# The order of the first loads, and two branch chunks moved behind a recurrence's last product

## The chip, the cores and the metric

The kernel runs on one core of a Trainium2 chip. The metric is the device time of one execution in microseconds (us); lower is better. The profile comes from one execution recorded by the hardware profiler; its engines are TensorE (PE, with its weight loads PEld), VectorE (DVE), ScalarE (ACT), GpSimd (POOL) and SyncE (SP), which here only issues DMAs.

## The reference

One layer of a hybrid encoder on x of 1024 rows by 1024 channels and a memory of 256 rows, all in float32:

```
h = rmsnorm(x);  z = h @ w_in                       # one projection, split into
(hq, hf, hi, hg, fq, fk, fv, ff, mq, gate_logits)   # parts of three mixers and three gates
y_a = hgrn2(hq, hf, hi, hg)      # gated linear recurrence, 4 heads, 128 x 128 state
y_b = fox(fq, fk, fv, ff)        # forgetting attention, 8 heads x 64, causal
y_c = memory_attention(mq, rmsnorm(mem) @ mem_kv_w) # 4 heads x 128 over 256 rows
merged = sum over b of sigmoid(gate_b) * (y_b @ w_br_b)
x = x + merged @ w_out
x = x + conv_glu_ffn(rmsnorm(x)) # up 1024 -> 2 x 2816, causal conv of 3, gelu, down
```

The recurrence's output is normalised per row and head and multiplied by silu(hg).

## The kernel before

Activations lie transposed: 128 channels on the partitions, the 1024 rows of the sequence along the free dimension, in eight tiles `xk[0]` to `xk[7]`. A float32 product is made from three TensorE products (`mm3`): both operands are split into a high part (a cast by ScalarE, L120, or L276 for x with its norm gain) and a low part (a subtraction by VectorE, L128 or L277), and high-high, high-low and low-high are added in PSUM (L114, L115, L116). One such product has 128 x 128 weights and 512 columns.

**The first part.** SyncE issues all loads in the order of the program. Memory (`mt`, 1 MB, transposed), the key-value weights of the memory (`wkv[0]` to `wkv[7]`, 512 KB each; 0 to 3 are for keys, 4 to 7 for values), x, the weights of the first two gate chunks (`rgw`, 512 KB each), and the rows of memory and of x, which are only needed for the sums of squares of the norms. The computing steps go by a list written out by hand, `SEQ`:

- `k0` to `k7` (`kv_chunk`): split one chunk of key-value weights, then 12 products on the normed memory; the result of the keys lies in two `tr` banks of PSUM, that of the values in two `pp` banks.
- `x0` to `x7` (`x_chunk`): scale and split 128 channels of x into `uh` and `ul`.
- `g0`, `g1` (`gate_weights`): split the weights of a gate chunk.
- `s0` to `s7` (`gate_step`): 12 products of both gate chunks on one channel tile of x.
- `mn` (`mem_norm`), `mk` (`mem_keys`): the keys are normed by ScalarE and VectorE (L326 to L331), turned by eight transposes (L336) and evicted into `mkf` (L338). `mv` (`mem_values`): ScalarE evicts the values from PSUM into `mvf` (L318).
- `xn` (`x_norm`): eight squares with sums by ScalarE, one for each row tile of x (L356), then the reciprocal root.

Behind the list comes the stream of dense projections. It uses banks of the same PSUM pools: `pp` has three, `tr` and `lg` two, `po` one. After the splits ScalarE also rescales the tiles of x (L542) in eight steps for a Strassen-like family of products; four are tied to the last split of x (`late["x_cast"]`), four to the last square (`late["square"]`).

A scheduler decides the order on each engine from priorities; the program's order is the base, and `tc.issue_after(ins)` ties instructions behind another one.

**The recurrence and the branches.** `hgrn_mix(h, ya)` runs one head in two halves of 512 rows (n = 0, 1). A half has a preparation (transposes of `kE`, L1033, products L1038), the products with the running state (L1044, L1046, with the states updated by VectorE at L1050 and L1052), and then `finish`: a square (L1060), a sum (L1061), four scalings by ScalarE (L1064), four transposes (L1067) and the multiplication by the gate (L1068). `state["last"]` is the last product with the state. A `finish` is held over and called inside the next half; the last one is called by the main program.

`branch(br, yh, yl, js)` projects a mixer's output: each chunk j is 24 products (two halves of the sequence, four channel tiles, three products each) whose result is multiplied by the gate (L1135) into `merged`. `weave` takes steps of several generators in turn, by their fractions done; `chain`, `held` and `ahead` join generators and give them priorities. The lines that the change meets are:

```
weave((ahead(hgrn_mix(3, ya), AHEAD), HGRN_STEPS), (chain(branch(1, yh, yl, range(2)), held(branch(1, yh, yl, range(2, 7)), 2)), 14))
state.pop("finish")()
with tc.issue_after(state["last"].ins):
    run_all(branch(1, yh, yl, (7,)))
```

So chunks 0 to 6 of branch 1 are woven with head 3 of the recurrence, and chunk 7 is tied behind its last product.

Of the kernel before, what the change touches and what calls it, by code (L numbers as in the profile page):

```python
# [8 lines left out]
F32 = mybir.dt.float32  # L9
# [25 lines left out]

FOX_STEPS, HGRN_STEPS, MEM_STEPS = 28, 14, 7
AHEAD = 300
FOX_LATE = 0.2  # L40
SEQ = ("k0 k1 k2 k3 x0 x1 g0 x2 mr g1 k4 s0 s1 x3 s2 k5 x4 mn mk s3 k6 x5 s4 k7 mv x6 s5 x7 xn s6 s7").split()
TMIN = -(1.0 - 2.0 ** -24)


# [13 lines left out]
def weave(*parts):  # L58

    live = [[g, max(n, 1), s[0] if s else 0.0, 0] for g, n, *s in parts]  # L60
    while live:
        p = min(live, key=lambda q: q[2] + (1.0 - q[2]) * q[3] / q[1])
        try:
            next(p[0])
            p[3] += 1
        except StopIteration:
            live.remove(p)
# [3 lines left out]
def tile_block(ctx: ExitStack, tc: tile.TileContext, xT, memT, x_rows, mem_rows, vec, fbias, mats, hmask, w_cm, w_hi, w_fqk, w_fv,  # L71
# [26 lines left out]
    def col(i):  # L98
        return cv[:, i:i + 1]


    def ahead(gen, offset):

        while True:
            with tc.high_priority(offset) if offset else nullcontext():
                try:
                    next(gen)
                except StopIteration:
                    return
            yield  # L110

    def mm3(ps, lh, ll, rh, rl, first, last, more=False):

        PE.matmul(ps, lh, rh, start=first, stop=False, skip_group_check=more)  # L114
        PE.matmul(ps, lh, rl, start=False, stop=False, skip_group_check=more)  # L115
        PE.matmul(ps, ll, rh, start=False, stop=last, skip_group_check=more)  # L116

    def cast(eng, out, in_):
        if eng is S:
# [6 lines left out]
    def split(eng, h, l, src, sub=None):  # L126
        cast(eng, h, src)
        return (sub or V).tensor_sub(l, src, h.bitcast(F32))  # L128

    def rstd_small(out, ss, n):  # L130
        w = ss.shape[1]
        V.tensor_scalar(out, ss, 1.0 / n, EPS, ALU.mult, ALU.add)
        return G.tensor_tensor(out, out, mhalf[:, :w], ALU.pow)
# [3 lines left out]
    def raw_weights(src, n):  # L137
        raw = wp.tile([P, 4 * 264], F32, tag="raw", name="raw", bufs=2)
        SP.dma_start(raw[:, :n], src)
        return raw  # L140

    def weights(src, shape, raw=None, hl=None, parts=1):

        n = shape[0] * shape[1]
        if raw is None:
            raw = raw_weights(src, n)
        if hl is None:
            hl = [wp.tile([P, 4 * 264], F32R, tag=t, name=t, bufs=3) for t in ("wh", "wl")]
        for i in range(parts):
            sl = slice(i * n // parts, (i + 1) * n // parts)  # L150
            split(wsplit[0], hl[0][:, sl], hl[1][:, sl], raw[:, sl], wsplit[1])
        return [t[:, :n].rearrange("p (a b) -> p a b", a=shape[0]) for t in hl]
# [43 lines left out]
    def row_tile(name):  # L196
        return p0.tile([P, 2 * HB], F32, tag="wkv", name=name, bufs=6)

    wkv = [row_tile(f"wkv{q}") for q in range(4)]
    mem_row = [row_tile(f"mr{i}") for i in range(2)]  # L200
    wkv += [row_tile(f"wkv{q}") for q in range(4, 8)]
    x_row = [row_tile(f"xr{i}") for i in range(6)]
    x_row += [row_tile(f"xr{i}") for i in (6, 7)]
    SP.dma_start(cv, vec)
    for q in range(4):
        w = 2 if q else 1
        for i in range(2 // w):
            sl, ws = slice(2 * q + i, 2 * q + i + w), slice(i * HB, (i + w) * HB)
            SP.dma_start(mt[:, sl, :], memT[:, sl, :])
            SP.dma_start(wkv[q][:, ws], w_mkv[q][:, ws])  # L210
    SP.dma_start(ones, mats[:, P:2 * P])
    rgw = []
    for what in SEQ:
        if what[0] == "x" and what != "xn":
            k = int(what[1])
            SP.dma_start(xk[k], xT[:, k, :])
        elif what == "mr":
            for i in range(2):
                SP.dma_start(mem_row[i], mem_rows[i])
        elif what[0] == "g":  # L220
            br, j = order[int(what[1])]
            rgw.append(raw_weights(w_cm[16 + 8 * br + j], KC * P))
        elif what in ("k4", "k5", "k6", "k7"):
            q = int(what[1])
            SP.dma_start(wkv[q], w_mkv[q])
    SP.dma_start(ident, mats[:, 0:P])
    for i in range(8):
        last_row = SP.dma_start(x_row[i], x_rows[i])
    G.memset(mhalf, -0.5)
    warm = cp.tile([P, 1], F32, tag="warm", name="warm")  # L230
    S.activation(warm, mhalf[:, 0:1], AF.Exp)
# [29 lines left out]

    umh = p0.tile([P, KC, NM], F32R, tag="umh", name="umh")
    uml = p0.tile([P, KC, NM], F32R, tag="uml", name="uml")
    for k in range(KC):
        S.activation(umh[:, k, :], mt[:, k, :], AF.Copy, scale=col(C_GM + k))
        V.scalar_tensor_tensor(out=uml[:, k, :], in0=mt[:, k, :], scalar=col(C_GM + k),
                               in1=umh[:, k, :].bitcast(F32), op0=ALU.mult, op1=ALU.subtract)
    rm = p0.tile([P, 2], F32, tag="rm", name="rm")

    def mem_norm():  # L270
# [2 lines left out]
        rstd_small(rm, rm, D)  # L273

    def x_chunk(k):
        late["x_cast"] = S.activation(uh[k], xk[k], AF.Copy, scale=col(C_GX + k))  # L276
        V.scalar_tensor_tensor(out=ul[k], in0=xk[k], scalar=col(C_GX + k), in1=uh[k].bitcast(F32),  # L277
                               op0=ALU.mult, op1=ALU.subtract)

    def spread_dma(r, rcol, pool, name):  # L280

# [22 lines left out]
    def kv_chunk(i):  # L304

        what, q = i // 4, i % 4
        if q == 0:
            pkv[what] = [ps_proj(), ps_proj()] if what else [ps_tr(), ps_tr()]
        wh, wl = weights(None, (2, HB), wkv[i], parts=1 if i else 2)
        for kk in range(2):  # L310
            k = 2 * q + kk
            for m in range(2):
                ms = slice(m * P, (m + 1) * P)
                mm3(pkv[what][m], umh[:, k, ms], uml[:, k, ms], wh[:, kk, :], wl[:, kk, :], k == 0, k == KC - 1)
# [27 lines left out]
    gw, gps = [], []  # L342

    def gate_weights(i):
        gw.append(weights(None, (KC, P), rgw[i], [p0.tile([P, KC * P], F32R, tag=t, name=t) for t in (f"gh{i}", f"gl{i}")]))
        gps.append([ps_proj(), ps_po()] if i else [ps_lg(), ps_lg()])

    def gate_step(k):
# [2 lines left out]
                sl = slice(n * HB, (n + 1) * HB)  # L351
                mm3(gps[i][n], gw[i][0][:, k, :], gw[i][1][:, k, :], uh[k][:, sl], ul[k][:, sl], k == 0, k == KC - 1)

    def x_norm():
        for i in range(8):
            late["square"] = S.activation(x_row[i], x_row[i], AF.Square, accum_out=rt[:, i:i + 1])  # L356
        rstd_small(rt, rt, D)

    steps = dict(k=kv_chunk, x=x_chunk, g=gate_weights, s=gate_step)
    named = dict(mn=mem_norm, mk=mem_keys, mv=mem_values, xn=x_norm)  # L360
    for what in SEQ:
        if what == "mr":
            continue
        if what in named:
            named[what]()
        else:
            steps[what[0]](int(what[1]))
    p0.release()

    home = {}  # L370
# [560 lines left out]
    def hgrn_mix(h, ya):  # L931
# [7 lines left out]
        for n in range(2):  # L939
# [113 lines left out]
                                               op0=ALU.mult, op1=ALU.add)  # L1053
                    St = Sn

            def finish(po=po, gz=gz, sl=sl):

                o2 = ph.tile([P, 4, P], F32, tag="o2", name="o2")
                rr = ph.tile([P, 4], F32, tag="rr", name="rr", bufs=2)
                S.activation(o2, po.rearrange("p (b v) -> p b v", b=4), AF.Square)  # L1060
                V.reduce_sum(rr, o2, axis=AX.X)  # L1061
                state["norm"] = rstd_small(rr, rr, 4 * P)
                for b in range(4):
                    S.activation(o2[:, b, :], po[:, b * P:(b + 1) * P], AF.Copy, scale=rr[:, b:b + 1])  # L1064
                ptr = ps_tr()
                for b in range(4):
                    PE.transpose(ptr[:, b * P:(b + 1) * P], o2[:, b, :], ident)  # L1067
                V.scalar_tensor_tensor(out=ya[:, h, sl], in0=ptr, scalar=hgc, in1=gz[:, sl], op0=ALU.mult, op1=ALU.mult)  # L1068

            state["finish"] = finish  # L1070
# [53 lines left out]
    def branch(br, yh, yl, js=range(8)):  # L1124
        for j in js:
            i = order.index((br, j))
            gts = []
            for n in range(2):
                gt = gate_tile()
                SP.dma_start(gt, gd[i, n])  # L1130
                gts.append(gt)
            for n, ps in br_chunk(br, j, yh, yl):
                dst = merged(j, n)
                if i < 8:
                    V.scalar_tensor_tensor(out=dst, in0=gts[n], scalar=1.0, in1=ps, op0=ALU.add, op1=ALU.mult)  # L1135
                else:
                    V.scalar_tensor_tensor(out=gts[n], in0=gts[n], scalar=1.0, in1=ps, op0=ALU.add, op1=ALU.mult)
                    V.tensor_add(dst, dst, gts[n])
                yield

    weave((ahead(hgrn_mix(3, ya), AHEAD), HGRN_STEPS), (chain(branch(1, yh, yl, range(2)), held(branch(1, yh, yl, range(2, 7)), 2)), 14))
    state.pop("finish")()
    with tc.issue_after(state["last"].ins):
        run_all(branch(1, yh, yl, (7,)))
    state["ph"].release()
# [509 lines left out]
```

## Time and profile before

| | us |
|---|---|
| median of 3 runs (lowest, highest) | 1734.2 (1732.5, 1734.95) |
| the profiled execution | 1735.67 |
| its span on the core | 1733.9 |
| TensorE busy | 1714.0 |
| VectorE busy | 1144.5 |
| ScalarE busy | 808.3 |
| GpSimd busy | 322.8 |

The span is what the timeline shows; 1.77 us of the profiled execution lie outside it. A row of the timeline gives start, duration, engine, line, operation, the tiles written and read, shapes and count, and in brackets how long the engine was idle before it and which engine, tile and line released it. "SPq" is the issue of a DMA. Where several rows overlap on one engine, the distance of their starts is what each one costs.

### The profile page before, as it was taken

Reading aid. Unit: us, or ns where it says so; the run is one execution under the profiler, and the core shown is the slowest. Engines: PE = TensorE matmul, PEld = TensorE weight load, DVE = VectorE, ACT = ScalarE, POOL = GpSimd, SP = SyncE. Lnnn points to the kernel's source line nnn. Section 1 sums busy time; section 2 is a strip of 40 time slices with the busy share of each in tenths; the row PEclk is TensorE's granted clock in tenths of the full one; section 3 lists DMA queues with packets and bytes.
Section 4 is the critical chain, followed back from the end, with each engine's and each line's share of the span. In section 5 each row is a group of like instructions: output and inputs, shape, how many; then the busy total and the mean of one; then the engine's idle time right before and its main releaser. Section 6 shows DMA issues by size and latency. Waiting matters only on the chain.

```text
span 1733.9 us, 24255 instructions
## 1 busy us (share of the span) xinstructions
PE 1714.0 (99%) x8941; PEld 1452.6 (84%) x8941; DVE 1144.5 (66%) x2046; ACT 808.3 (47%) x1436; POOL 322.8 (19%) x417
## 2 busy tenths in 40 slices
PE   8999999999999999999989999999999999999998
PEld 6778899989898998888878888788888888888887
DVE  7656545665666564886856745987777787765654
ACT  8634346645454553776531333644334344433332
POOL 0100022443433331544210000211111111100000
PEclk9999999999999999999999999999999999999999
DMA  9533142221212111100336542565445345494772
GB/s 358 179 123 115 66 137 86 76 90 44 98 62 79 55 50 56 61 31 24 111 113 199 162 182 97 158 172 168 138 148 140 116 133 152 159 348 157 249 264 85
DMA packets 83207, 227.23 MB, mean 131 GB/s; under 512 B 9600, under 2 KB 12424, under 8 KB 83088
## 3 DMA queue, kind: packets, MB, share of 16 engines
q1 hardware_dynamic: 65040, 161.19, 26.8%
q0 software_dynamic: 18048, 64.50, 12.8%
q8 instruction: 70, 1.15, 0.3%
q14 instruction: 49, 0.40, 0.1%
HBM read 180.78 MB, written 67.93 MB: 143 GB/s over the span
## 4 chain that ended last, share of the span: by engine, by line
PE 96%; DMA 2%; DVE 1%; SPq 0%; issue 0%; ACT 0%; POOL 0%; DVEq 0%; POOLq 0%; ACTq 0%
PE pp L116 21%; PE pp L115 21%; PE pp L114 21%; PE lg L116 4%; PE lg L115 4%; PE lg L114 4%; PE tr L115 2%; PE tr L116 2%; PE tr L114 2%; PE po L836 1%; PE lg L795 1%; PE lg L794 1%; PE po L835 1%; PE po L116 1%; PE po L114 1%; PE po L115 1%
## 5 line engine op out<-in xcount | busy, mean ns | idle before, releaser
L116 PE MATMUL pp<-uh,wl 128*128 128x512 f32 x412 | 164.4, 399 | 0.0
L115 PE MATMUL pp<-ul,wh 128*128 128x512 f32 x412 | 164.4, 399 | 0.0
L114 PE MATMUL pp<-uh,wh 128*128 128x512 f32 x412 | 163.6, 397 | 0.0
L115 PE MATMUL pp<-wl,uh 128*128 128x256 f32 (+1 forms) x512 | 145.9, 286 | 0.0
L116 PE MATMUL pp<-wh,ul 128*128 128x256 f32 (+1 forms) x512 | 145.6, 285 | 0.0
L114 PE MATMUL pp<-wh,uh 128*128 128x256 f32 (+1 forms) x512 | 145.1, 285 | 0.0
L120 ACT CAST wh<-s 128x512 fp32r<-128x512 f32 x113 | 68.3, 619 | 157.7 <-PE pp L115 84.9
L120 ACT CAST wh<-raw 128x1024 fp32r<-128x1024 f32 (+2 forms) x76 | 67.6, 890 | 111.6 <-PE pp L115 95.5
L120 ACT CAST wh<-rw 128x512 fp32r<-128x512 f32 x87 | 53.2, 619 | 104.7 <-PE pp L115 62.1
L1300 POOL DMA_DIRECT2D rw<-in_w_up x44 | 24.2, 556 | 399.4 <-DVE wl L1193 178.4
L114 PEld LDWEIGHTS pp<-wh,uh 128*128 128x128 f32 x512 | 96.7, 189 | 1.2
L116 PEld LDWEIGHTS pp<-wh,ul 128*128 128x128 f32 x512 | 96.8, 189 | 0.9
L115 PEld LDWEIGHTS pp<-wl,uh 128*128 128x128 f32 x512 | 96.7, 189 | 0.9
L128 DVE TENSOR_TENSOR wl<-raw,wh 128x1024 fp32r<-128x1024 f32 (+2 forms) x75 | 78.1, 1041 | 28.8 <-ACT wh L120 28.3
L120 ACT CAST dwh<-wr 128x1024 fp32r<-128x1024 f32 (+1 forms) x41 | 40.1, 979 | 118.5 <-PE tr L115 39.7
L114 PEld LDWEIGHTS pp<-uh,wh 128*128 128x128 f32 x412 | 78.0, 189 | 15.7 <-ACT wh L120 0.3
L115 PEld LDWEIGHTS pp<-ul,wh 128*128 128x128 f32 x412 | 77.5, 188 | 15.8
L116 PEld LDWEIGHTS pp<-uh,wl 128*128 128x128 f32 x412 | 77.5, 188 | 15.7
L128 DVE TENSOR_TENSOR dwl<-wr,dwh 128x1024 fp32r<-128x1024 f32 (+1 forms) x41 | 46.3, 1129 | 34.0 <-ACT dwh L120 33.9
L810 ACT ACTIVATE pt<-pt,st 128x128 f32<-128x128 f32 (+3 forms) x64 | 49.7, 777 | 40.0 <-DVE st L807 33.1
L812 POOL TENSOR_SCALAR pt<-pt,st 128x128 f32<-128x128 f32 (+3 forms) x64 | 51.1, 798 | 78.0 <-DVE st L811 59.9
L120 ACT CAST ph<-tr 128x512 fp32r<-128x512 f32 (+1 forms) x80 | 41.7, 544 | 39.8 <-PE tr L824 17.6
(500 smaller groups left out, 5145.3 us busy)
## 6 DMA issues: line engine op xcount, KB each, us to landing
rw<-in_w_up POOLq DMA_DIRECT2D x44, 512.0 KB, 4.6
sd<-in_w_dn POOLq DMA_DIRECT2D x30, 512.0 KB, 5.9
br<-yd SPq DMA_DIRECT2D x30, 512.0 KB, 5.3
raw<-in_w_cm SPq DMA_DIRECT2D x26, 512.0 KB, 3.4
gd<-gt SPq DMA_DIRECT2D x48, 256.0 KB, 2.0
gt<-gd SPq DMA_DIRECT2D x48, 256.0 KB, 2.7
yd<-fc SPq DMA_DIRECT2D x44, 256.0 KB, 2.4
wr<-sd SPq DMA_DIRECT2D x20, 512.0 KB, 5.0
```

The costliest lines, as they stand in the source:

```text
L114: PE.matmul(ps, lh, rh, start=first, stop=False, skip_group_check=more)
L115: PE.matmul(ps, lh, rl, start=False, stop=False, skip_group_check=more)
L116: PE.matmul(ps, ll, rh, start=False, stop=last, skip_group_check=more)
L120: return S.copy(out, in_)
L128: return (sub or V).tensor_sub(l, src, h.bitcast(F32))
L794: PE.matmul(ps[:, :w], qa[i][:, tsl], kh[i][:, s0:s0 + w], start=True, stop=False)
L795: fox_sets[p][3] = PE.matmul(ps[:, :w], qa[i][:, tsl], kl[i][:, s0:s0 + w], start=False, stop=True)
L810: S.activation(pt[:, :ns], pt[:, :ns], AF.Exp, bias=st[:, 2:3], accum_out=st[:, 3:4])
L812: G.tensor_scalar(pt[:, :ns], pt[:, :ns], st[:, 3:4], 0.0, ALU.mult, ALU.add)
L835: PE.matmul(o, vhl[:, sb, :], ph[:, src], start=(sb == 0), stop=False)
L836: PE.matmul(o, vhl[:, sb, :], pl[:, src], start=False, stop=last)
L1300: late["raw"] = G.dma_start(raw[:, 2 * i:2 * i + 2, :], src[:, 2 * i:2 * i + 2, :])
```

## The change

The first loads come in a new order, written as a list of its own (`LOADS`): gate weights and channels of x, then the memory, its rows, the key-value weights and the rows of x. The computing list `SEQ` follows: all eight gate steps first, then the memory's operand, the eight key-value chunks and the norms. The first gate's weights and the first tile of x are loaded and split in two pieces each (256 and 768 columns; 512 and 512), the first key-value chunk in one instead of two. The squares of x are single steps in the list. In the other place chunk 6 of branch 1 leaves the weave and is issued behind the recurrence's last product, and the last four transposes of `finish` are tied behind chunk 6's last product (`late["mm"]`, kept by `mm3`); chunk 7 follows as before.

```diff
-SEQ = ("k0 k1 k2 k3 x0 x1 g0 x2 mr g1 k4 s0 s1 x3 s2 k5 x4 mn mk s3 k6 x5 s4 k7 mv x6 s5 x7 xn s6 s7").split()
+LOADS = "g0 x0 g1 x1 x2 x3 x4 x5 x6 x7 m mr k0 k1 k2 k3 k4 k5 xr0 xr1 xr2 xr3 k6 k7 xr4 xr5 xr6 xr7".split()
+SEQ = ("g0 x0 g1 s0 x1 s1 x2 s2 x3 s3 x4 s4 x5 s5 x6 s6 x7 s7 m k0 mn k1 k2 k3 k4 xr0 k5 xr1 xr2 mk xr3 k6 xr4 k7 xr5 "
+       "mv xr6 xr7 xn").split()
...
-        PE.matmul(ps, ll, rh, start=False, stop=last, skip_group_check=more)
+        late["mm"] = PE.matmul(ps, ll, rh, start=False, stop=last, skip_group_check=more)
...
+    for what in LOADS:
+        i = int(what[-1]) if what[-1].isdigit() else None
+        if what[:2] == "xr":
+            x_row[i] = row_tile(what)
+            last_row = SP.dma_start(x_row[i], x_rows[i])
+        elif what[0] == "x":
+
+            sl = slice(0 if i else HB, T)
+            SP.dma_start(xk[i][:, sl], xT[:, i, sl])
+        elif what[0] == "g":
+            br, j = order[i]
+            rgw[i] = wp.tile([P, 4 * 264], F32, tag="raw", name="raw", bufs=2)
+            for sl in (slice(0, 2 * P), slice(2 * P, KC * P)) if i == 0 else (slice(0, KC * P),):
+                SP.dma_start(rgw[i][:, sl], w_cm[16 + 8 * br + j][:, sl])
+                if i == 0 and sl.start == 0:
+                    SP.dma_start(xk[0][:, :HB], xT[:, 0, :HB])
...
-    def x_norm():
-        for i in range(8):
-            late["square"] = S.activation(x_row[i], x_row[i], AF.Square, accum_out=rt[:, i:i + 1])
-        rstd_small(rt, rt, D)
+    def x_square(i):
+        late["square"] = S.activation(x_row[i], x_row[i], AF.Square, accum_out=rt[:, i:i + 1])
...
-            def finish(po=po, gz=gz, sl=sl):
+            def finish(after=None, po=po, gz=gz, sl=sl):
...
-                for b in range(4):
-                    PE.transpose(ptr[:, b * P:(b + 1) * P], o2[:, b, :], ident)
+                with tc.issue_after(after.ins) if after is not None else nullcontext():
+                    for b in range(4):
+                        PE.transpose(ptr[:, b * P:(b + 1) * P], o2[:, b, :], ident)
...
-    weave((ahead(hgrn_mix(3, ya), AHEAD), HGRN_STEPS), (chain(branch(1, yh, yl, range(2)), held(branch(1, yh, yl, range(2, 7)), 2)), 14))
-    state.pop("finish")()
+    weave((ahead(hgrn_mix(3, ya), AHEAD), HGRN_STEPS), (chain(branch(1, yh, yl, range(2)), held(branch(1, yh, yl, range(2, 6)), 2)), 12))
+
+    with tc.issue_after(state["last"].ins):
+        run_all(branch(1, yh, yl, (6,)))
+    state.pop("finish")(late["mm"])
     with tc.issue_after(state["last"].ins):
         run_all(branch(1, yh, yl, (7,)))
```

More of the change, by code (lines that the diff above doesn't have):

```diff
@@ L197, in row_tile @@
         return p0.tile([P, 2 * HB], F32, tag="wkv", name=name, bufs=6)
[L199 to L203, printed above, removed]
-    SP.dma_start(cv, vec)
[L205 to L216, printed above, removed]
+    wkv, mem_row, x_row, rgw = {}, {}, {}, {}
+    SP.dma_start(cv, vec)
+    for what in LOADS:
[13 more added lines that the diff above has]
+                    SP.dma_start(xk[0][:, :HB], xT[:, 0, :HB])
+        elif what == "m":
+            for sl in (slice(0, 4), slice(4, 8)):
+                SP.dma_start(mt[:, sl, :], memT[:, sl, :])
@@ L217, in tile_block @@
         elif what == "mr":
             for i in range(2):
+                mem_row[i] = row_tile(f"mr{i}")
                 SP.dma_start(mem_row[i], mem_rows[i])
[L220 to L225, printed above, removed]
+            SP.dma_start(ones, mats[:, P:2 * P])
+        else:
+            wkv[i] = row_tile(what)
+            SP.dma_start(wkv[i], w_mkv[i])
@@ L226, in tile_block @@
     SP.dma_start(ident, mats[:, 0:P])
-    for i in range(8):
-        last_row = SP.dma_start(x_row[i], x_rows[i])
     G.memset(mhalf, -0.5)
@@ L263, in tile_block, with memory_operand @@
     uml = p0.tile([P, KC, NM], F32R, tag="uml", name="uml")
[L264 to L267, printed above, removed]
+    def memory_operand():
+        for k in range(KC):
+            S.activation(umh[:, k, :], mt[:, k, :], AF.Copy, scale=col(C_GM + k))
+            V.scalar_tensor_tensor(out=uml[:, k, :], in0=mt[:, k, :], scalar=col(C_GM + k),
+                                   in1=umh[:, k, :].bitcast(F32), op0=ALU.mult, op1=ALU.subtract)
     rm = p0.tile([P, 2], F32, tag="rm", name="rm")
@@ L275, in x_chunk @@
     def x_chunk(k):
-        late["x_cast"] = S.activation(uh[k], xk[k], AF.Copy, scale=col(C_GX + k))
-        V.scalar_tensor_tensor(out=ul[k], in0=xk[k], scalar=col(C_GX + k), in1=uh[k].bitcast(F32),
-                               op0=ALU.mult, op1=ALU.subtract)
+        for sl in [slice(0, HB), slice(HB, T)] if k == 0 else [slice(0, T)]:
+            late["x_cast"] = S.activation(uh[k][:, sl], xk[k][:, sl], AF.Copy, scale=col(C_GX + k))
+            V.scalar_tensor_tensor(out=ul[k][:, sl], in0=xk[k][:, sl], scalar=col(C_GX + k),
+                                   in1=uh[k][:, sl].bitcast(F32), op0=ALU.mult, op1=ALU.subtract)
     def spread_dma(r, rcol, pool, name):
@@ L308, in kv_chunk @@
             pkv[what] = [ps_proj(), ps_proj()] if what else [ps_tr(), ps_tr()]
-        wh, wl = weights(None, (2, HB), wkv[i], parts=1 if i else 2)
+        wh, wl = weights(None, (2, HB), wkv[i])
         for kk in range(2):
@@ L344, in gate_weights @@
     def gate_weights(i):
-        gw.append(weights(None, (KC, P), rgw[i], [p0.tile([P, KC * P], F32R, tag=t, name=t) for t in (f"gh{i}", f"gl{i}")]))
+        hl = [p0.tile([P, KC * P], F32R, tag=t, name=t) for t in (f"gh{i}", f"gl{i}")]
+        for sl in (slice(0, 2 * P), slice(2 * P, KC * P)) if i == 0 else (slice(0, KC * P),):
+            split(S, hl[0][:, sl], hl[1][:, sl], rgw[i][:, sl])
+        gw.append([t.rearrange("p (a b) -> p a b", a=KC) for t in hl])
         gps.append([ps_proj(), ps_po()] if i else [ps_lg(), ps_lg()])
@@ L352, in gate_step @@
                 mm3(gps[i][n], gw[i][0][:, k, :], gw[i][1][:, k, :], uh[k][:, sl], ul[k][:, sl], k == 0, k == KC - 1)
-    def x_norm():
-        for i in range(8):
-            late["square"] = S.activation(x_row[i], x_row[i], AF.Square, accum_out=rt[:, i:i + 1])
-        rstd_small(rt, rt, D)
-    steps = dict(k=kv_chunk, x=x_chunk, g=gate_weights, s=gate_step)
-    named = dict(mn=mem_norm, mk=mem_keys, mv=mem_values, xn=x_norm)
+    def x_square(i):
+        late["square"] = S.activation(x_row[i], x_row[i], AF.Square, accum_out=rt[:, i:i + 1])
+    steps = dict(k=kv_chunk, x=x_chunk, g=gate_weights, s=gate_step, xr=x_square)
+    named = dict(m=memory_operand, mn=mem_norm, mk=mem_keys, mv=mem_values, xn=lambda: rstd_small(rt, rt, D))
     for what in SEQ:
-        if what == "mr":
-            continue
         if what in named:
@@ L366, in tile_block @@
         else:
-            steps[what[0]](int(what[1]))
+            steps[what[:-1]](int(what[-1]))
     p0.release()
```

## The prediction

> **What bounds the kernel now.** I read the page's span and busy lines first, then TensorE's waits, then the timeline around the two places that the change touches.
>
> ```profile
> span 1733.9 us, 24255 instructions
> ...
> PE 1714.0 (99%) x8941; PEld 1452.6 (84%) x8941; DVE 1144.5 (66%) x2046; ACT 808.3 (47%) x1436; POOL 322.8 (19%) x417
> ```
> ```profile
> PE tr L114 <- ACT wh L120: 6.4, 2, 5.2
> PE tr L1067 <- ACT o L1064: 3.9, 1, 3.9
> PE pp L116 <- DVE fa L1392: 1.7, 1, 1.7
> ```
>
> TensorE is busy for 1714.0 of 1733.9 us, so 19.9 us is all that any reordering of unchanged work can win. The waits say where those lie: 6.4 us at the start (5.2 before the first product and one more), 3.9 us at L1067, 1.7 us in the FFN, which the change does not touch. A reader should see two things: the change touches the first two places, and everything else that it moves lies where TensorE does not wait today, so that it can only lose there.
>
> The profiled execution took 1735.67 us, 1.47 above the median of the runs (1734.2). I make the sum against the span and add it to the median.
>
> **The start.** The number of products before the dense projections is the same before and after (96 for the gates, 96 for keys and values, 8 transposes). What counts is how late TensorE runs against an uninterrupted stream.
>
> ```profile
> 2.58 0.43 SPq L210 DMA_DIRECT2D wkv<-in_w_mkv  x1
> 3.06 0.43 SPq L209 DMA_DIRECT2D mt<-in_memT  x1
> 3.53 0.43 SPq L210 DMA_DIRECT2D wkv<-in_w_mkv  x1
> ...
> 5.18 1.22 PE L114 MATMUL tr<-wh,umh 128*128 128x512 f32 x2 [5.18 <-ACT wh L120]
> ...
> 6.36 0.62 ACT L120 CAST wh<-wkv 128x512 fp32r<-128x512 f32 x1 [0.82 <-DMA wkv<-in_w_mkv]
> ...
> 7.05 0.63 PE L115 MATMUL tr<-wl,umh 128*128 128x512 f32 x1
> ...
> 7.48 0.63 PE L116 MATMUL tr<-wh,uml 128*128 128x512 f32 x1
> ...
> 8.56 0.91 ACT L265 ACTIVATE umh<-mt,cv 128x256 fp32r<-128x256 f32 x2 [1.58 <-DMA mt<-in_memT]
> ...
> 9.83 1.04 ACT L120 CAST wh<-wkv 128x1024 fp32r<-128x1024 f32 x1 [0.36 <-DMA wkv<-in_w_mkv]
> ...
> 10.91 1.23 DVE L128 TENSOR_TENSOR wl<-wkv,wh 128x1024 fp32r<-128x1024 f32 x1 [0.92 <-ACT wh L120]
> 10.93 0.74 PE L114 MATMUL tr<-wh,umh 128*128 128x512 f32 x2 [1.17 <-ACT wh L120]
> ...
> 12.19 0.50 PE L115 MATMUL tr<-wl,umh 128*128 128x512 f32 x1 [0.52 <-DVE wl L128]
> ...
> 25.26 0.50 PE L116 MATMUL po<-uh,gl 128*128 128x512 f32 x1 [0.27 <-DVE gl L128]
> ```
>
> The unit of the stream is below: twelve 512-wide products start at 52.30 and the thirteenth at 55.11, so 2.81 us for twelve and 0.234 for one. At 12.19 fourteen products are done, worth 3.28 us; TensorE has then lost 12.19 − 3.28 = 8.91 us, and 0.27 more at 25.26: 9.2 us.
>
> In the changed kernel the first loads are gate weights 128 KB, half of x's first channels 256 KB, the rest of the weights 384 KB, the other half 256 KB, then the second gate's weights 512 KB. Before they are 128, 256, 128, 256, 256 and 512 KB of memory and key weights. So at equal bytes the first product is cast as early (5.2), the fourth product waits for what 1 MB brings (before, 8.56), and the second gate's weights come with 1.5 MB (cast at 9.83, its low part subtracted 10.91 to 12.14). The built order on TensorE is six products of gate 0, then four of gate 1 that need no low part, then two that do. So ten products are done at 12.2 where before fourteen were: the loss is 12.19 − 10 × 0.234 = 9.85 us, **0.7 later**. Bounds: each load of equal bytes is issued one slot earlier (2.58, 3.06 and 3.53 are 0.47 apart), and if the chain follows that and the 0.27 is not met again elsewhere, the start is 0.9 earlier; if the clock, cold at first (7.05 to 7.48 is 0.43 for one product against 0.234), stays cold for some 3.5 us longer because TensorE now idles between the third product and the fourth, it is 0.7 + 1.7 = 2.4 later. I take +0.7, since the bytes are equal.
>
> **The end of this part.** Here is the term that I think decides. Before, the last steps were gate steps; the eviction of the memory values (L318) ran under them. After, the key and value chunks are last.
>
> ```profile
> 23.88 1.27 ACT L326 ACTIVATE mkt<-tr,rm 128x512 f32<-128x512 f32 x2
> 25.04 1.04 ACT L120 CAST wh<-wkv 128x1024 fp32r<-128x1024 f32 x1
> 25.97 1.16 ACT L327 ACTIVATE mkt<-mkt 128x512 f32<-128x512 f32 x2
> ...
> 46.59 1.04 ACT L356 ACTIVATE xr<-xr 128x1024 f32<-128x1024 f32 x1
> ...
> 47.63 1.04 ACT L356 ACTIVATE xr<-xr 128x1024 f32<-128x1024 f32 x1
> ...
> 48.67 0.67 ACT L318 ACTIVATE mvf<-pp,rm 128x512 f32<-128x512 f32 x1
> ...
> 54.41 4.25 ACT L542 ACTIVATE xk<-xk,cv 128x1024 f32<-128x1024 f32 x4
> ```
> ```profile
> 37.92 1.04 PE L336 MATMUL tr<-ident,mkt 128*128 128x128 f32 x8
> 38.72 0.48 PE L116 MATMUL pp<-wh,uml 128*128 128x512 f32 x1
> ...
> 52.30 0.39 PE L114 MATMUL lg<-uh,gh 128*128 128x512 f32 x1
> ...
> 55.11 0.39 PE L114 MATMUL pp<-uh,wh 128*128 128x512 f32 x1
> ```
>
> The product at 55.11 is the first of the dense projections. In the changed kernel its PSUM bank is that of the first value half, so it waits for ScalarE's first L318. ScalarE works in order, and in the built kernel its order from the end of the fourth key chunk on is (lines of the kernel before):
>
> ```
> L326 mkt x2 (needs the fourth key chunk's products)
> L356 square; L327 x2; L120 cast k6, k7; L356; L120 raw
> L356 x2; L120 raw; L356
> L542 rescale of x, channels 4 to 7
> L318 mvf x2
> ```
>
> By the rows that is 1.16 (L326, 23.88 to 25.04) + 5 × 1.04 (squares) + 1.16 (L327) + 4 × 0.93 (casts, 25.04 to 25.97) + 4.25 (L542) + 0.67 (the first L318) = **16.2 us**. TensorE meanwhile has four value chunks of twelve products, 11.2 us, and the eight transposes, 0.80 (37.92 to 38.72): **12.0 us**. So it waits 16.2 − 12.0 = **4.2 us** where before it waited for nothing (the row at 55.11 has no wait). ScalarE itself is not late before this chain: from 11 us to the chain's start at 9.85 + 144 × 0.234 = 43.6 it has some 26 us of casts and squares. Bounds: rows overlap by about 0.1 each, and the scheduler's list is fixed, so 3.5; 5.0 if a row of x comes late. Behind the waiting product, TensorE's whole dense stream is queued, so all of it is paid. The eviction of the keys (L338) and the transposes of the row norms come after, under that stream, at no cost as long as it covers them; uncovered it would be two evictions, 1.3 us, in the upper bound.
>
> **What the wait does to the clock.** The trace has one idle time of this size, and one short one.
>
> ```profile
> 889.20:893.60 4.40, 0.48 (x4) 0.25 (x3) 2.72 (x6) 1.77 (x5) 1.01 (x1) 0.89 0.39 119
> 893.57:899.97 6.40, 5.96 (x29) 5.67 (x30) 1.79 (x4) 1.20 (x4) 0.00 (x0) 0.54 0.00 0
> ```
>
> These are windows of all engines; the columns are length, busy time of TensorE, its weight loads, VectorE, ScalarE and GpSimd, then granted clock. While TensorE idles the mean clock is 0.89, and after it 0.54: 3.92 us of idling cost the clock about (1 − 0.54) × 6.4 = 2.9 us. The 1.17 us at 10.93 did not (its stream goes on at full pitch after 12.19). A wait of 4.2 us is nearest to the first. I take +1.7: half of 3.5 us of cold stream, the length of the start's cold stretch, since here a dense stream follows at once; bounds 0 (clock kept) and 2.9.
>
> The Trainium skill ("TensorE: Matmul & The Clock Gate", Part 1, the HAM clock gate) says that the clock halves only after a whole idle window of about 3.4 us and that these windows run freely, whatever the kernel does. By that an idle time of 4.2 us holds a whole window only in about (4.2 − 3.4) / 3.4, a quarter, of its positions, and the sum would more often be 1.7 lower; the trace's one case of 3.92 us did drop.
>
> **The branch part.** The weave now holds chunks 0 to 5 of branch 1, and chunk 6's 24 products go behind the recurrence's last product (L1046 of the last half), the last four transposes behind these, then chunk 7.
>
> ```profile
> 882.48 0.48 PE L116 MATMUL pp<-yh,wl 128*128 128x512 f32 x1
> ...
> 889.26 0.38 PE L1046 MATMUL po<-St,qe 128*128 128x128 f32 x2
> 893.57 0.48 PE L1067 MATMUL tr<-ident,o 128*128 128x128 f32 x1 [3.92 <-ACT o L1064]
> ...
> 906.52 0.60 PE L1067 MATMUL tr<-ident,o 128*128 128x128 f32 x4
> ```
> ```profile
> 882.99 0.69 DVE L1135 SCALAR_TENSOR_TENSOR mgl<-gt,pp 128x512 f32<-128x512 f32 x1
> 883.60 0.68 DVE L128 TENSOR_TENSOR wl<-raw,wh 128x512 fp32r<-128x512 f32 x1
> 884.20 0.34 DVE L1052 SCALAR_TENSOR_TENSOR St<-St,eg,tr 128x128 f32<-128x128 f32 x1
> ...
> 890.67 0.68 DVE L1061 TENSOR_REDUCE rr<-o 128x4 f32<-128x512 f32 x1
> ```
> ```profile
> 889.74 0.60 ACT L1060 ACTIVATE o<-po 128x512 f32<-128x512 f32 x1 [0.34 <-PE po L1046]
> ```
>
> L1067 occurs twice. The wait of 3.92 us at 893.57 belongs to the *first* half of head 3; the recurrence's products of the second half follow it. The last transposes are those at 906.52, and they have no wait: chunk 7 already covers them. So chunk 6 gains nothing at its new place. At its old place it lay between 882.79 and 889.2, between the last products of the first half, and covered their chain of states on VectorE. Without it the last product would start 24 × 0.234 = 5.6 earlier, at 883.65; but VectorE starts the first state (L1052) at 884.20, behind L1135 and L128, and three of them at 0.34 less some overlap end at about 885.1. So it starts some 1.4 later than the move alone allows. The finishing chain behind (L1060, L1061) gains back up to 0.3, as L1061, ready at 889.74 + 0.60 = 890.34, had to wait until 890.67 for VectorE. Net **+1.1**: TensorE idles about as long in all, no work having come to the stall. Bounds: 0 and +2; and if the idle time in one piece falls to 3.6 us and the clock stays up, the 2.9 us above come back: −1.8.
>
> **Sum.** 0.7 + 4.2 + 1.7 + 1.1 = +7.7 us: 1734.2 + 7.7 = **1741.9 us**.
>
> **Rivals.** *No cold clock at either place:* 0.7 + 4.2 + 1.1 − 2.9 = +3.1, 1737.3. For it: 4.2 and 3.6 us are close to what the one observed drop needed; against it, that drop. *All upper bounds:* start 2.4, wait 5.0, clock 2.0, branch 1.1: +10.5, 1744.7. *The other side:* ScalarE reaches L318 in time. It decides at the four rescalings: if they do not stand ahead of L318 in effect (because the squares before them finish under earlier idle time), the chain is 16.2 − 4.25 = 12.0 us, as long as TensorE's, and there is neither wait nor drop. Then +1.8 remains, 1736.0; with the branch's clock kept, −1.1, 1733.1; with the start's early bound too, −2.7, 1731.5. Against it: ScalarE's order is fixed in the built kernel, and L326 cannot start before the fourth key chunk ends. *The change does not do what it says:* the last transposes had no wait to cover; that is in the sum already.
>
> **How the numbers follow.** Some 0.2%, 3.5 us, is what a measurement of this kernel can tell from no change. Forecast, with or without one of the two clock terms (+4.8 to +7.7): 0.64, slower. Upper bounds (+9 to +11): 0.10, slower. No cold clock anywhere (+2 to +3.5): 0.16, the same. ScalarE in time: 0.10, of it 0.08 the same and 0.02 faster; faster gets 0.03 with the chance of something unseen, the same 0.23. The range leaves out most of the last case and the top of the upper bounds: 1736.0 to 1745.5.
>
> **What would show it.** In the profile after, TensorE's waits would list the first dense product (pp, L114 of before) on ScalarE's mvf with about 4 us, a granted clock near one half right behind it, L1067 with 3.5 to 4 us still there, and ten products done at about 12.2 us. If the mvf wait is under 1 us, the forecast is wrong at its main term; if L1067's wait is gone or under 2 us, at the branch.

## The result, and the profile after

| | before | after |
|---|---|---|
| median of 6 runs, us | 1733.8 (1732.5 to 1734.95) | 1739.79 (1739.29 to 1740.68) |
| the profiled execution, its span | 1735.67, 1733.9 | 1739.85, 1738.1 |

The changed kernel is slower: the ratio is 1.0035, 95% interval 1.0022 to 1.0048, that is 3.8 to 8.3 us; the medians differ by 6.0. The forecast was +7.7, 1741.9 with a range of 1736.0 to 1745.5.

The page after, and TensorE's waits after (engine, product and line, what released it: us in total, times, longest). Lines of the changed kernel stand three to ten higher than before: L117 to L119 are the three products, L325 is the value eviction, L548 the rescaling of x, L1074 the transposes of the recurrence's output.

```profile
span 1738.1 us, 24251 instructions
...
PE 1714.7 (99%) x8941; PEld 1451.9 (84%) x8941; DVE 1144.5 (66%) x2047; ACT 808.5 (47%) x1437; POOL 324.4 (19%) x417
```
```profile
PE lg L117 <- ACT uh L283: 6.7, 2, 5.3
PE pp L117 <- ACT mvf L325: 4.3, 1, 4.3
PE tr L1074 <- ACT o L1070: 3.6, 1, 3.6
PE pp L119 <- DVE fa L1402: 1.6, 1, 1.6
PE po L1052 <- DVE St L1058: 1.2, 2, 0.8
```

TensorE does the same work (1714.7 against 1714.0). The list of waits has one new large line, the value eviction, and the wait at the recurrence's transposes is still there: 3.6 us instead of 3.9.

The new wait, on ScalarE and on TensorE:

```profile
44.27 1.25 ACT L333 ACTIVATE mkt<-tr,rm 128x512 f32<-128x512 f32 x2
...
55.45 4.25 ACT L548 ACTIVATE xk<-xk,cv 128x1024 f32<-128x1024 f32 x4
59.60 1.24 ACT L325 ACTIVATE mvf<-pp,rm 128x512 f32<-128x512 f32 x2
```
```profile
55.02 1.03 PE L343 MATMUL tr<-ident,mkt 128*128 128x128 f32 x8
60.32 0.51 PE L117 MATMUL pp<-uh,wh 128*128 128x512 f32 x1 [4.27 <-ACT mvf L325]
```

The rows of ScalarE from 44.27 to 59.60 follow each other without a pause. From the first read of the keys out of PSUM at 44.27 (L333) until the first value eviction is done and TensorE starts at 60.32 it takes 16.05 us, where 16.2 was forecast. The four rescalings stand right ahead of the eviction. TensorE is through with its chunks and transposes at 56.05.

The clock behind this wait, in windows of all engines (length, busy time of TensorE, weight loads, VectorE, ScalarE and GpSimd, granted clock, DMA share, GB/s):

```profile
56.05:60.32 4.27, 0.01 (x1) 0.00 (x0) 0.00 (x0) 4.27 (x6) 2.22 (x2) 1.00 0.63 224
60.32:60.70 0.38, 0.38 (x2) 0.33 (x3) 0.00 (x0) 0.38 (x1) 0.00 (x0) 1.00 0.03 11
60.70:64.10 3.40, 3.40 (x10) 2.63 (x9) 1.29 (x2) 3.40 (x8) 1.12 (x2) 0.52 0.51 196
64.10:64.50 0.40, 0.40 (x3) 0.37 (x2) 0.00 (x0) 0.40 (x2) 0.00 (x0) 0.84 1.02 419
```

The clock is full while TensorE idles and for the first 0.4 us of work after it; then it is half for some 3.4 us. That costs 3.4 × (1 − 0.52) = 1.6 us.

### The profile page after: what moved, and what is told of

Its sections match the earlier page's. It is cut to its first block, busy times and chain, and to the rows that moved or that the text cites. A ratio compares the mean times of both kernels' runs of the same rounds, so it can differ in the third digit from the quotient of the medians.

```text
span 1738.1 us, 24251 instructions
## 1 busy us (share of the span) xinstructions
PE 1714.7 (99%) x8941; PEld 1451.9 (84%) x8941; DVE 1144.5 (66%) x2047; ACT 808.5 (47%) x1437; POOL 324.4 (19%) x417
## 4 chain that ended last, share of the span: by engine, by line
PE 96%; ACT 1%; DMA 1%; DVE 1%; issue 0%; POOL 0%; SPq 0%; DVEq 0%; ACTq 0%; POOLq 0%
PE pp L119 21%; PE pp L118 21%; PE pp L117 21%; PE lg L118 4%; PE lg L117 4%; PE lg L119 4%; PE tr L118 3%; PE tr L119 3%; PE tr L117 3%; PE po L842 1%; PE lg L801 1%; PE lg L800 1%; PE po L841 1%; PE po L117 1%; PE po L118 1%; PE po L119 1%
## 5 line engine op out<-in xcount | busy, mean ns | idle before, releaser
L117 PE MATMUL pp<-uh,wh 128*128 128x512 f32 x412 | 164.2, 399 | 4.3 <-ACT mvf L325 4.3
L119 PE MATMUL pp<-uh,wl 128*128 128x512 f32 x412 | 165.0, 401 | 0.0
L119 PE MATMUL pp<-wh,ul 128*128 128x256 f32 (+1 forms) x512 | 145.3, 284 | 0.0
L117 PE MATMUL pp<-wh,uh 128*128 128x256 f32 (+1 forms) x512 | 144.7, 284 | 0.0
L117 PEld LDWEIGHTS pp<-wh,uh 128*128 128x128 f32 x512 | 96.4, 189 | 1.2
L119 PEld LDWEIGHTS pp<-wh,ul 128*128 128x128 f32 x512 | 96.5, 189 | 0.9
L117 PEld LDWEIGHTS pp<-uh,wh 128*128 128x128 f32 x412 | 78.5, 190 | 20.3 <-ACT mvf L325 4.5
L119 PEld LDWEIGHTS pp<-uh,wl 128*128 128x128 f32 x412 | 77.8, 189 | 15.6
```

What stands on the lines that cost most here:

```text
L119: late["mm"] = PE.matmul(ps, ll, rh, start=False, stop=last, skip_group_check=more)
```

## The experiments

Each was timed in five rounds beside the kernel before on the same chip. Differences are against that kernel's median in the same comparison.

**The start alone.** Edit of the changed kernel:

```diff
-    weave(... held(branch(1, yh, yl, range(2, 6)), 2)), 12))
-
-    with tc.issue_after(state["last"].ins):
-        run_all(branch(1, yh, yl, (6,)))
-    state.pop("finish")(late["mm"])
+    weave(... held(branch(1, yh, yl, range(2, 7)), 2)), 14))
+    state.pop("finish")()
```

> The changed kernel with its branch part undone (chunk 6 back in the weave, the last transposes untied); the new loads and the new order of the first part stay. Theory (the first part carries the loss: ScalarE's late eviction of the values stops TensorE for 4.3 us, the clock then runs at half for one stretch, 1.7 us): the time stays within 1 us of the changed kernel, 1739 to 1740.5, +5 to +6.5 on the kernel before, and the wait on mvf stays at 4 to 4.5 us. Rival (the branch part carries its forecast +1.1 us or more): 1738.7 or less.

Measured 1739.82 against 1733.38: +6.4, ratio 1.0032 (1.0021 to 1.0043), and the wait is the same:

```profile
PE pp L117 <- ACT mvf L325: 4.3, 1, 4.3
PE tr L1074 <- ACT o L1070: 3.9, 1, 3.9
```

The first part carries the loss: it alone costs as much as the whole change (+6.4 and +6.0).

**The branch part alone**, put into the kernel before (chunk 7 stood behind the last product already, so chunk 6 is the one that moves):

```diff
... (late["mm"] and finish(after) as in the change; the weave holds chunks 0 to 5)
-    state.pop("finish")()
+    with tc.issue_after(state["last"].ins):
+        run_all(branch(1, yh, yl, (6,)))
+    state.pop("finish")(late["mm"])
```

> The kernel before with only the branch part of the change (chunk 6 behind the recurrence's last product, the last transposes behind it). Theory: the wait at the first half's transposes stays at 3.6 to 3.9 us, and the time moves by 0 to +1.1 us, 1733.8 to 1734.9. Rival (the move covers something that waited): 1731 or less, with the wait on the scaled output under 2 us.

Measured 1734.48 against 1733.38: +1.1, ratio 1.0005 (0.9997 to 1.0014), so between −0.5 and +2.4 us. Its waits:

```profile
PE tr L1068 <- ACT o L1064: 3.6, 1, 3.6
PE pp L116 <- DVE fa L1396: 1.6, 1, 1.6
PE po L1046 <- DVE St L1052: 1.2, 2, 0.8
```

The wait at the first half's transposes stays and the waits for the states (L1052) grow from 0.4 to 1.2 us; the move covers nothing that waited. A gain of 2 us or more is excluded, a loss of 1 us is likely but not shown by the times.

**The evictions ahead of the rescalings.** In the changed kernel, with `late["mk"]` the last key eviction:

```diff
-with tc.issue_after(late["square" if t > 3 else "x_cast"].ins):
+with tc.issue_after(late["mk" if t > 3 else "x_cast"].ins):
```

> The changed kernel, with the four rescalings of x, channels 4 to 7, tied behind the evictions of values and keys instead of behind the last square. Theory: the first value eviction then starts about when the four squares and casts before it end, 55.5 us, and TensorE waits under 0.6 us for it; without the long wait the clock stays up. That gives back 4.0 + 1.7 us: 1733.5 to 1734.7. Rival (the loss lies in the start, in the loads or in the branch part): the wait goes and the time stays above 1737.

Measured 1735.46 against 1733.38: +2.1, ratio 1.0010 (1.0002 to 1.0019). The wait on the value eviction is gone and the clock stays up there, and about 4 of the 6 us come back, where 5.7 were expected; the time fits neither the theory nor the rival (above 1737). Of what is left, 1.2 us is a new wait, for a weight cast, at 92.60 us; the 0.7 us below it was there before the change too (0.7) and in the changed kernel (0.8).

```profile
PE pp L117 <- ACT wh L123: 1.2, 1, 1.2
PE pp L117 <- ACT fe L433: 0.7, 1, 0.7
```

**Two of the four rescalings ahead of the evictions** (`"mk" if t > 5 else "square" if t > 3 else "x_cast"`).

> The changed kernel with two of the four rescalings (channels 6 and 7) behind the evictions and two still ahead. Theory: the wait on mvf falls by two rescalings, 2.1 us, to 2.1 to 2.3 us. If an idle time of 2.2 us costs no clock, the time falls by 2.1 + 1.7 = 3.8 us, to about 1736.0; if it does, only by 2.1, to 1737.7, with the granted clock at one half behind the wait. Rival for the price of the clock (a cold stretch costs nothing in the dense stream): 1737.7 with the clock up.

Measured 1738.28 against 1733.38: +4.9, ratio 1.0025 (1.0015 to 1.0036). The interval, +2.6 to +6.2, leaves out the first number (+2.2) and holds the second (+3.9). In the profile (an execution of 1741.02 us, the slowest of its seven) there are two waits of 2.2 us:

```profile
PE pp L117 <- ACT fe L433: 2.2, 1, 2.2
PE pp L117 <- ACT mvf L325: 2.2, 1, 2.2
```

The wait on mvf fell as worked out. The other, at 91.08 us, is on a later copy by ScalarE (L433), for which the changed kernel waits 0.8. Behind the wait on mvf the clock stayed up (the products are 0.23 us apart from 58.20 on); at 91 us it did not:

```profile
88.89:91.08 2.19, 0.01 (x1) 0.01 (x1) 2.19 (x5) 2.19 (x6) 0.00 (x0) 0.99 0.81 322
91.08:91.50 0.42, 0.42 (x1) 0.42 (x2) 0.42 (x1) 0.42 (x2) 0.00 (x0) 0.50 0.47 59
...
92.00:95.00 3.00, 3.00 (x9) 2.33 (x8) 3.00 (x6) 1.59 (x4) 0.00 (x0) 0.59 0.90 311
```

Two idle times of 2.19 us in one execution, one with and one without a cold stretch: the length alone does not decide.

**Work in place of the idle time.** The key transposes move behind the value evictions in the program (a step `mt` of their own behind `mv`), and four of them are repeated ten times (`FILL = 11`):

```diff
...
-            for h in range(2):
+            for h in [0, 1] * (FILL if hh else 1):
                 for m in range(2):
                     PE.transpose(ptr[:, (2 * h + m) * P:(2 * h + m + 1) * P],
```

> The changed kernel, with four of the eight transposes of the keys repeated ten times more (40 extra transposes into the same bank with the same result, some 4 us) while ScalarE is on its way to the value evictions; ScalarE's order up to these evictions is unchanged. Nothing comes earlier: the first dense product still starts at about 60.3 us. Theory (behind the idle time the clock costs 1.7 us by itself): TensorE's clock stays up and the time falls by 1.5 to 1.9 us against the changed kernel, to about 1738. Rival (the slow products behind the wait are hidden by something else that is late): no fall, 1739.5 to 1740.

Measured 1738.02 against 1732.99: +5.0, ratio 1.0028 (1.0018 to 1.0039). That is 1.0 us nearer to the kernel before than the changed kernel is, but the intervals overlap, so the times alone don't settle it. The trace of one execution (1739.19 us, the slowest of the eight) does for the clock:

```profile
55.70:61.10 5.40, 5.40 (x50) 5.24 (x48) 0.81 (x2) 5.40 (x8) 2.23 (x2) 1.00 0.57 197
61.10:65.00 3.90, 3.90 (x18) 3.17 (x18) 1.49 (x3) 2.63 (x5) 1.12 (x2) 1.00 0.34 134
```

The clock is 1.00 throughout. From the first dense product to the first product of the family T2, its wait taken off, TensorE needs 31.03 us (61.02 to 93.24, less 1.19) against 32.58 in the changed kernel (60.32 to 93.72, less 0.82): 1.55 us less. In this execution the start was 0.7 later (transposes at 55.71 instead of 55.02); whether the others started late too, so that the median fell by 1.0 only, was not traced.

**The cover where the idle time is.** In the kernel before, with chunk 6 out of the weave:

```diff
                     if H == 64 and "finish" in state:
-                        state.pop("finish")()
+                        if h == 3 and n == 1:
+                            with tc.issue_after(state["last"].ins):
+                                run_all(branch(1, yh, yl, (6,)))
+                            state.pop("finish")(late["mm"])
+                        else:
+                            state.pop("finish")()
```

> The kernel before, with chunk 6 of branch 1 tied behind the last product of the first half of head 3, and that half's transposes behind chunk 6: the idle time of 3.9 us in the profile is there, not at the last transposes. Theory: that wait goes to under 0.5 us and the clock stays up, worth 3.9 + 1.7 to 3.4 us, less up to 1.4 us because the chain of states on VectorE is no longer covered by chunk 6: 4 to 6 us faster than before, 1727.5 to 1729.5. Rival (another step of the chain, such as the second half's first products, is late by as much): 1732 or more, with the wait under another name.

Measured 1729.22 against 1732.99: −3.8, ratio 0.9977 (0.9968 to 0.9987). The gain is clear of noise, though a little under the 4 to 6 us of the theory. The wait on the scaled output has left the list; what is new is 1.2 us on VectorE's mask of the next half. The clock did not stay up as expected: in the trace it is at one half from 866.6 to 870.0, for 3.4 us, where before it was so for 6.8 (892.6 to 899.4). The waits:

```profile
PE tr L114 <- ACT wh L120: 6.5, 2, 5.4
PE lg L1018 <- DVE A L1021: 1.2, 1, 1.2
PE pp L114 <- ACT fe L427: 0.7, 1, 0.7
```

**The rescalings behind the casts of T1**, in the changed kernel (`late["t1"]` is the last of these casts):

```diff
...
-                with tc.issue_after(late["square" if t > 3 else "x_cast"].ins):
+        for t in range(4, 8):
+            with tc.issue_after(late["t1"].ins):
+                S.activation(xk[t], xk[t], AF.Copy, scale=col(C_GX + t))
```

> The changed kernel with the four rescalings of x, channels 4 to 7, behind the four casts of the first family (T1), so behind the value and key evictions and two weight casts too. Theory: the wait on mvf is gone as in the version with the rescalings right behind the evictions, and of what that version still lost (a wait of 1.2 us on a weight cast near 92 us) part goes too; what remains is the later start, about 1 us: 1733.8 to 1735. Rival (ScalarE has no slack anywhere in this stretch, so 4.2 us of rescaling are paid wherever they stand): 1736 or more, with a wait on ScalarE of 2 us or more further on.

Measured 1736.47 against 1732.99: +3.5, ratio 1.0022 (1.0013 to 1.0031). The rival's time (1736 or more) was met, its wait of 2 us on ScalarE was not: the wait on L433 grew from 0.8 to 1.8 us, and one of 0.9 us on VectorE (L387) is new. The 1.6 us in the FFN are as in the changed kernel.

```profile
PE pp L117 <- ACT fe L433: 1.8, 1, 1.8
PE pp L119 <- DVE fa L1404: 1.6, 1, 1.6
...
PE pp L117 <- DVE gt L387: 0.9, 1, 0.9
```

**The rescalings in ScalarE's idle time.** In the changed kernel ScalarE stood idle before the chain, waiting for TensorE to free a weight buffer:

```profile
28.74 2.93 ACT L123 CAST wh<-k 128x1024 fp32r<-128x1024 f32 x3
35.66 1.05 ACT L123 CAST wh<-k 128x1024 fp32r<-128x1024 f32 x1 [3.99 <-PE tr L119]
```
```diff
...
-with tc.issue_after(late["square" if t > 3 else "x_cast"].ins):
+with tc.issue_after(late["k2" if t > 3 else "x_cast"].ins):
```

> The changed kernel with the four rescalings of x, channels 4 to 7, tied behind the cast of the third key chunk, that is into the 4.0 us from 31.7 to 35.7 us in which ScalarE stands idle in the changed kernel (it waits there for a free weight buffer). Nothing else of ScalarE's order moves. Theory: the wait on mvf goes to zero, the clock stays up, and as no work is pushed behind the evictions, no wait of 1 us or more on ScalarE appears before 95 us; what is left against the kernel before is the start, 0.9 us, and the branch part, 0 to 1.1 us: 1733.9 to 1735.2. Rival (the versions with later rescalings lost 2 to 3.5 us for another reason than ScalarE's backlog): 1735.5 or more.

Measured 1735.04 against 1732.72: +2.3, ratio 1.0009 (1.0000 to 1.0018). The rescalings fill the gap, and between the first product and 95 us neither a wait on mvf nor one over 0.7 us on ScalarE is left. The time does not separate theory and rival: +2.3 is a little over the theory's 0.9 to 2.0, whose upper part lies in the interval (0 to 3.1), and it is no better than the version with the evictions first (+2.1), which had the wait of 1.2 us.

```profile
31.28 4.26 ACT L549 ACTIVATE xk<-xk,cv 128x1024 f32<-128x1024 f32 x4
35.62 1.05 ACT L123 CAST wh<-k 128x1024 fp32r<-128x1024 f32 x1
```
```profile
PE lg L117 <- ACT uh L283: 5.7, 1, 5.7
PE tr L1075 <- ACT o L1071: 3.6, 1, 3.6
...
PE pp L117 <- ACT fe L434: 0.7, 1, 0.7
```

**Both edits together**, the rescalings in the gap and the cover at the first half:

> The same, and instead of the change's branch part chunk 6 behind the last product of the first half of head 3, where the idle time is. Theory: the two edits add up, 1729.0 (the cover on the kernel before) plus the later start of 0.9 us, 1729.3 to 1730.8. Rival (the cold stretches of the clock move with the phase so that gains of the two places don't add up): 1731.5 or more.

Measured 1728.1 against 1732.72: −4.6, ratio 0.9969 (0.9959 to 0.9980), lower than the theory's 1729.3; why, the runs do not show. From the cover on the kernel before (0.9977) it cannot be told apart; both are faster than either kernel of this case.

## Why the prediction was right

**The main term, 4.2 us for the late value eviction: right, 4.27.** The order of ScalarE and its path of 16.2 us (16.05) held. The agreement to 0.1 is closer than the working: the path began 0.48 behind the last key product (43.79 to 44.27, a square ran first), and TensorE's work took 12.26 (43.79 to 56.05) instead of 12.0, so 0.48 + 16.05 − 12.26 = 4.27. That the four rescalings decide it was the rival's condition, and the runs show it from both sides: with the rescalings elsewhere the wait is gone, with two of them ahead it is 2.19.

**The start, +0.7: right in size, 0.9, in part by luck.** The first dense product could start at 60.32 − 4.27 = 56.05 instead of 55.11. The steps were as worked out, with one difference:

```profile
8.69 0.80 PE L117 MATMUL lg<-uh,gh 128*128 128x512 f32 x1 [1.36 <-ACT uh L283]
...
12.25 0.63 PE L119 MATMUL pp<-uh,gl 128*128 128x512 f32 x1
12.68 0.56 PE L119 MATMUL po<-uh,gl 128*128 128x512 f32 x1
13.08 0.63 PE L117 MATMUL lg<-uh,gh 128*128 128x512 f32 x2
13.55 0.40 PE L117 MATMUL pp<-uh,gh 128*128 128x512 f32 x1
```
```profile
9.28 1.05 ACT L123 CAST gh<-raw 128x1024 fp32r<-128x1024 f32 x1 [0.65 <-DMA raw<-in_w_cm]
10.36 1.23 DVE L131 TENSOR_TENSOR gl<-raw,gh 128x1024 fp32r<-128x1024 f32 x1 [0.94 <-ACT gh L123]
```

Ten products are done at 12.25, as forecast, but from another cause. The second gate's weights came earlier (cast at 9.28, not 9.83), so their low part was there at 11.59 and TensorE does not wait for it; instead it works at the cold pitch of 0.43 until about 13.1. The longer cold stretch that was named as an upper bound came, and the earlier weights hid much of it: two misses of opposite sign.

**The clock, +1.7: right in size, 1.6 in the trace and 1.55 by the filled wait.** The length taken from the start's cold stretch, 3.5 us, held (3.4). What decides whether the clock falls was not known: the prediction went by one case of 3.92 us, and the two traces with this wait (changed kernel and start alone) agree with it, but the version with two rescalings shows that the position counts too. Without this term the sum would be 6.0, just what was measured. That is chance: the cold stretch is in the trace.

**The branch part, +1.1: not settled.** Alone it measured +1.1, with an interval from −0.5 to +2.4. In the changed kernel's trace the states were late as worked out, and the idle time fell by the 0.3 that L1061 gains:

```profile
888.88 1.27 DVE L1058 SCALAR_TENSOR_TENSOR St<-St,eg,tr 128x128 f32<-128x128 f32 x3
```

The three states end at 890.15, and TensorE waited 0.15 + 0.78 us for the states: 0.6 us more idle time in all, where 1.4 − 0.3 was forecast. From a point ahead of it to one behind it the two profiled executions drifted apart by only 0.2 us, from 4.7 (transposes, 244.31 to 249.03) to 4.9 (FFN, 1106.89 to 1111.79), and the cold stretch behind the idle time was half as long:

```profile
892.70:899.40 6.70, 5.39 (x24) 5.10 (x25) 1.69 (x4) 1.62 (x5) 0.41 (x1) 0.50 0.03 10
```
```profile
893.60:897.10 3.50, 3.24 (x15) 3.24 (x16) 0.75 (x1) 1.46 (x5) 0.00 (x0) 0.51 0.00 0
```

The first line is before, the second after. That is no gain of the change: of the seven traced versions with its branch part two have 3.4 us there and five 6.8. That the last transposes had nothing to cover, and that the wait belongs to the first half of the head, is shown by the cover placed there: 3.8 us gained.

**The sum was 1.7 too high**, 7.7 against 6.0, though 7.7 lies in the interval of the measurement (3.8 to 8.3), so the 1.7 is not clear of noise. In the one pair of traces three small terms differ from the forecast. A wait of 0.58 us for a weight's low part at 91.36 in the kernel before does not come after. The branch part cost 0.2, not 1.1. The last product starts 4.79 us later (1729.00 to 1733.79), but the span ends only 4.2 later, so the end behind it, with the last stores, took 0.6 less. With these, 0.9 + 4.3 + 1.6 − 0.6 + 0.2 − 0.6 = 5.8. The spans of this pair differ by only 4.2; the profiled execution of before held one more cold stretch, at 237 us, worth some 1.7, which the changed kernel's did not:

```profile
234.10:235.00 0.90, 0.04 (x2) 0.01 (x1) 0.00 (x0) 0.69 (x2) 0.00 (x0) 1.00 0.87 269
235.00:237.30 2.30, 2.30 (x19) 2.30 (x20) 1.22 (x1) 1.74 (x2) 0.00 (x0) 0.99 0.32 123
237.30:240.70 3.40, 3.40 (x19) 3.40 (x18) 2.61 (x3) 1.08 (x3) 0.00 (x0) 0.51 0.35 123
```

**The rivals.** "No cold clock" did not come, nor "ScalarE in time". "All upper bounds" was not quite that: it took 2.0 for the clock and 1.1 for the branch, whose bounds were 2.9 and 2; with these it would be 12.3 instead of 10.5. What no rival had is that rescalings moved back come up again further on, as waits of 1.2 us (evictions first) and 1.8 us (behind T1). ScalarE alone is not short of time there: from 74 to 92 us it is busy 10.85 and 11.69 of 18 us in these two versions and waits up to 4.8 us for VectorE, which is busy 17.01 and 18.00. So the delay probably runs through both engines; by which steps was not traced. And 19.9 us is not all that can be won: a cold stretch counts as busy time of TensorE.

## What to carry to other kernels

When loads or steps are reordered so that TensorE starts differently, follow the engine that evicts: work that was hidden under the last steps of the old order is exposed when other steps come last, and its in-order queue tells by how much. Work that stands ahead of a late eviction can go behind it, or into an idle time that the same engine has earlier. Here both took the wait away, and their times cannot be told apart (+2.1 and +2.3 us); only the second left no new wait on that engine. Before covering a wait, find which instance of the line waits: the same transposes occur for both halves of a head here, and only the first half's left TensorE idle.

## What the runs showed of the hardware

The clock falls and rises on a grid. The time of a fall can be read from the mean granted clock of a window: in the kernel before, 236 to 238 us has 0.81, so 0.76 us of it were at one half and the clock fell at 237.24. Read so:

| trace | fall at | and at | apart | in steps of 3.413 us |
|---|---|---|---|---|
| two rescalings ahead | 91.04 | 241.24 | 150.20 | 44.0 |
| before | 237.24 | 892.60 | 655.36 | 192.0 |
| changed kernel | 60.80 | 893.68 | 832.88 | 244.0 |
| start alone | 61.40 | 897.64 | 836.24 | 245.0 |

A single stretch lasts 3.40 to 3.44 (237.24 to 240.64, 60.80 to 64.24), so 150.20 can only be 44 steps, of 3.413 to 3.414 each; the larger distances then are whole numbers of the same step.

The idle time of 2.19 us that cost the clock in the version with two rescalings (88.89 to 91.08) ended where the clock fell, at 91.04. Ten steps earlier is 56.9, in the middle of the other idle time of 2.19 us (55.67 to 57.86), which cost nothing: neither of the two windows that it touches was idle for more than 1.3 us. This agrees with the Trainium skill ("TensorE: Matmul & The Clock Gate", Part 1, the HAM clock gate) in that the window is about 3.4 us long and runs freely. It does not agree that a whole window must be idle: 2.15 us of idling inside one window sufficed; in the changed kernel the window up to 60.80 held 0.5 us of work; and in the trace of before the window up to 237.24 held 0.86 us of idling and then 0.92 us of eight products of one column each. So an idle time of 2.2 us cost here either nothing more than its length or a cold stretch besides, some 1.6 us in a dense stream, by where it fell.
